# A second product scheme for w_down's other columns, in part of the rows, and plain steps into its banks

## The chip, the cores and the metric

The kernel runs on one core of a Trainium2 chip. The metric is the device time in microseconds; the kernel before takes 2009.6 us (median of 3 runs, 2009.06 to 2009.94). The engines are TensorE (PE: matmuls, PEld: its weight loads), VectorE (DVE), ScalarE (ACT), GpSimd (POOL) and SyncE (SP, which here only issues DMAs). Matmul sums land in PSUM banks of 128 x 512 fp32 values, from where DVE or ACT read them; the operands lie in SBUF.

## The reference

A two-layer bidirectional encoder over 256 tokens of width 2048, in fp32. Each layer has an attention part with three kinds of heads, and then the MLP, where this change is:

```
h = rmsnorm(x, norm_mlp[l])
u = relu(h @ w_up[l])          # 256 x 8192
x = x + (u * u) @ w_down[l]    # 8192 x 2048
```

## The kernel before

**Precision.** Each fp32 operand of a matmul is split into a high and a low part of the faster type fp32r. A product a·b is taken as three: high·high, low·high and high·low. For weights the split is made on the chip, step by step: ACT casts the tile to `whi` (L992), DVE subtracts to get `wlo` (L993).

**Steps.** Nearly all weight work is a list `steps`, one weight tile of 512 KB each, walked in order by the loop at the end of `tile_trunk`. At step i the loop issues the loads up to step i + 6 (`LOOK_LOAD`), the splits up to step i + 2 (in the MLP), the preparations `prep` up to step i + 4 (`LOOK_PREP`), and then the step's matmuls. `whi` and `wlo` have three buffers, the loaded tiles `wraw` five, `side` four, and `spare0` and `spare1` one each. The framework turns this into instructions for each engine, adds the waits, and may place an instruction that is ready ahead of one that isn't; so the order on an engine need not be the written one.

**The MLP in groups.** The 8192 inner columns are worked in eight groups g of 1024. `up_steps(g)` makes 16 steps that give the squared activations `uT[q]`, four tiles q per group with the high and the low part of 256 inner columns for all 256 tokens; an evaluation chain of ACT and DVE instructions follows every fourth step, and `sums_of` forms from the same values four sums of quarters, `sT[q]`, for the scheme below.

**Down in two ways.** The 2048 output columns fall into four blocks j of 512. For j = 2 and 3 `down_steps` is plain: per step 12 matmuls (two token halves t, two row blocks, three parts; `mode_b`, L465), into one bank per token half; after the group's last step DVE adds both banks to x (L720). For j = 0 and 1 `strassen_steps` uses seven products in place of eight (Winograd's form): the 2 x 2 block matrix has the two token halves as rows of the left side, two sets of inner rows between, and the columns j = 0 and j = 1 on the right. Each product P1 to P7 has two steps, for the two halves h of the group's rows, with 6 matmuls each (L787). The left operands are parts of `uT` (A11, A12, A22) or of `sT` (S1 to S4). The right operands come from the four weight blocks B11, B12, B21, B22:

- P1 loads B11 into a `spare` tile. As soon as it is split, an accumulating DMA issued from POOL adds B12 to it (`on_top`, in P2's `prep`).
- P2 takes B21 as it is.
- P7 loads B12 and B22 into `side` tiles; DVE adds them (L808).
- P6 takes B22 plus the spare tile, a DVE add (L814) into a `big` tile; when it is split, another accumulating DMA adds B21 (P5's `prep`). P4 takes that sum.
- P5 takes the spare tile, P3 takes B22.

The products share three banks. `a` and `d` are the halves of the one PSUM tile `S` that `score_banks()` gives (a new one is asked for at P1), `b` is an ordinary bank. P1, P6, P5 and P3 accumulate on in `a`, P7 and P4 in `d`, P2 is alone in `b`. Between the products DVE adds the state of the bank to, or subtracts it from, a quarter of x (`evac`, L763): once per product, at its second half.

**The order.** `order` merges the lists: 1 takes the next product step, 0 the next other step. In groups 0 to 5 the others are first 8 plain down steps (4 for j = 2, 4 for j = 3), then the 16 up steps of group g + 1. Each product stands as `1 0 1`, with two or three zeros up to the next product; two zeros come first. Groups 6 and 7 are ordered apart, and the last two groups' plain columns are done in group 7. A group of 0 to 5 has 38 steps.

Of the kernel before, what the change touches and what calls it, by code (L numbers as in the profile page):

```python
# [17 lines left out]
F32 = mybir.dt.float32  # L18
# [5 lines left out]
P = 128  # L24
# [19 lines left out]
def tile_trunk(ctx: ExitStack, tc: tile.TileContext, x_in, xt_in, w_in, w_o, w_up, w_down,  # L44
               gains, rowp, t5, rpb, gfin, cst, onehot, out):
    nc = tc.nc
    LOOK_LOAD, LOOK_SPLIT, LOOK_PREP, BUDGET = 7, 2, 5, 2.2
# [26 lines left out]
    def spare(dt, h):  # L74

        return wp.tile([P, 2, 512], dt, tag=f"spare{h}", bufs=1, name=nm("spare"))
# [4 lines left out]
    def mm_bank():  # L81
        return pp.tile([P, 512], F32, tag="bank", bufs=6, name=nm("mm"))
# [4 lines left out]
    def score_banks():  # L87
        return pp.tile([P, 4, 256], F32, tag="S", bufs=1, name=nm("S"))
# [5 lines left out]
    x = cp.tile([P, NT, D], F32, name="x")  # L94
# [356 lines left out]
    steps = []  # L451

    class Step:


        def __init__(self, src, kk, n, pre, mm, fourth=True, loads=None, prep=None, raw=None, post=None):
            self.src, self.kk, self.n, self.pre, self.mm, self.fourth = src, kk, n, pre, mm, fourth
            self.loads, self.prep, self.raw, self.post = loads or [], prep, raw, post

    def mode_b(banks, h_tile, wh, wl, sub, first, last, n=512, blocks=(0, 1), lo_last=False):  # L460

        def one(t, i, part):
            kk = sub[i]
            a = h_tile[i][:, int(part == "lh"), kk, t * P:(t + 1) * P]
            nc.tensor.matmul(banks[t][:, 0:n], a, (wl if part == "hl" else wh)[:, i, :],  # L465
                             start=first and i == 0 and part == "hh",
                             stop=last and i == len(sub) - 1 and part == stop)
        if lo_last:
            stop = "hl"
            for part in ("hh", "lh", "hl"):  # L470
                for t in blocks:
                    for i in range(len(sub)):
                        one(t, i, part)
            return
        stop = "lh"
        for t in blocks:
            for i in range(len(sub)):
                for part in ("hh", "hl", "lh"):
                    one(t, i, part)
# [3 lines left out]
    def layer_steps(l):  # L483
# [97 lines left out]
        ti = 0  # L581
# [114 lines left out]
            nc.vector.tensor_sub(t[:, 1], sm, f(t[:, 0]))  # L696
            sT[q] = t

        def down_steps(gs, j):

            out_, box = [], {}
            tiles = [(g, k) for g in gs for k in range(4)]
            final = l == L - 1 and gs == (7,)
            for n, (g, k) in enumerate(tiles):
                def mm(wh, wl, g=g, k=k, n=n):
                    last = n == len(tiles) - 1
                    if n == 0:
                        box["b"] = [mm_bank(), mm_bank()]
                        box["w"] = []
                    hts = [uT[4 * g + k]] * 2  # L710
                    mode_b(box["b"], hts, wh, wl, [0, 1], n == 0, last, blocks=(0,) if final else (0, 1),
                           lo_last=gs != (7,))
                    if final:
                        box["w"].append((hts, wh, wl))
                    if not last:
                        return

                    def evac(t):
                        xs = x[:, t, j * 512:(j + 1) * 512]
                        nc.vector.tensor_add(xs, xs, box["b"][t])  # L720
                    if final:
                        evac(0)
                        final_block(0)
                        tail = [mm_bank(), mm_bank()]
                        for c in range(2):
                            cols = slice(c * 256, c * 256 + 256)
                            for i, (hts, vh, vl) in enumerate(box["w"]):
                                mode_b([None, tail[c]], hts, vh[:, :, cols], vl[:, :, cols], [0, 1],
                                       i == 0, i == 3, n=256, blocks=(1,))
                            xs = x[:, 1, 1536 + c * 256:1792 + c * 256]  # L730
                            nc.vector.tensor_add(xs, xs, tail[c][:, 0:256])
                            square_cols(1, 1536 + c * 256, 256, fin["ss"][:, 7 + c:8 + c])
                        final_block(1)
                        return
                    evac(0)
                    evac(1)
                    if gs[-1] == 7:
                        layer_end(l, j)
                out_.append(Step(w_down[l, (g * 4 + j) * 4 + k], 2, 512, None, mm, fourth=gs == (7,)))
            return out_  # L740

        def strassen_steps(g):

# [2 lines left out]
            raw, t2, box, done = {}, {}, {}, set()  # L748

            def src(par, j, h):  # L750
                return w_down[l, g * 16 + (par * 2 + j) * 2 + h]

            def left(name, q):

# [3 lines left out]
                return [sT[q][:, i, "3124".index(name[1]), :] for i in range(2)]  # L758

            def evac(bank, t, j, sign):  # L760
                xs = x[:, t, j * 512:(j + 1) * 512]
                op = nc.vector.tensor_add if sign > 0 else nc.vector.tensor_sub
                op(xs, xs, bank)  # L763

# [8 lines left out]
                nc.gpsimd.dma_start(tile, src(par, j, h).rearrange("p (k n) -> p k n", k=2), accum_op=ALU.add)  # L773
            out_ = []
            for name, lf, bk, fresh, dst in plan:
                for h in range(2):
                    def mm(wh, wl, name=name, lf=lf, bk=bk, fresh=fresh, dst=dst, h=h):
                        if (name, h) == ("P1", 0):
                            pair = score_banks().rearrange("p (b i) n -> p b (i n)", i=2)
                            box["a"], box["d"] = pair[:, 0], pair[:, 1]  # L780
                        if (name, h) == ("P2", 0):
                            box["b"] = mm_bank()
                        o = box[bk]
                        ops = [left(lf, 2 * h + i + 4 * g) for i in range(2)]
                        for a, w in ((0, wh), (1, wh), (0, wl)):
                            for i in range(2):
                                nc.tensor.matmul(o, ops[i][a], w[:, i, :], skip_group_check=True,  # L787
                                                 start=fresh and h == 0 and i == 0 and a == 0 and w is wh,
                                                 stop=h == 1 and i == 1 and w is wl)
                        if h == 1:  # L790
                            evac(o, *dst)

                            if g == 7 and name in ("P3", "P4"):
                                layer_end(l, dst[1])
                    loads, prep, get = [], None, None
                    if name == "P1":
                        loads = [(("B11", h), src(0, 0, h), lambda h=h: spare(F32, h))]
                        get = lambda h=h: raw["B11", h]
                    elif name == "P2":
                        def prep(h=h):  # L800
# [25 lines left out]
                    def operand(get=get, key=(name, h)):  # L826
                        done.add(key)
                        return get()
                    stp = Step(src(1, 0, h) if name == "P2" else None, 2, 512, None, mm, fourth=False, prep=prep,
                               raw=operand if get else None,  # L830
                               loads=[(raw, k, v, w) for k, v, w in loads])
                    out_.append(stp)
            return out_

        steps.extend(up_steps(0))
        for g in range(8):

            if g < 6:
                ss = down_steps((g,), 2) + down_steps((g,), 3) + up_steps(g + 1)
            elif g == 6:  # L840
                ss = up_steps(7)
            else:
                ss = down_steps((6, 7), 2) + down_steps((6,), 3) + down_steps((7,), 3)
            hs = strassen_steps(g)

            order = [0, 0]
            for p_ in range(7):
                order += [1, 0, 1]
                if p_ < 6:
                    order += [0] * (2 if g < 6 else g == 6) + [0] * (g != 6 and p_ in (1, 3, 5))  # L850
            order += [0] * (len(ss) - order.count(0))
            assert order.count(0) == len(ss) and order.count(1) == len(hs), (order.count(0), order.count(1))
            steps.extend(hs.pop(0) if o else ss.pop(0) for o in order)

# [174 lines left out]
    for i, s in enumerate(steps):  # L1029
# [17 lines left out]
        while ns < min(len(steps), i + LOOK_SPLIT + (not s.fourth)):  # L1047
            split(ns)
            ns += 1
        while npr < min(len(steps), i + LOOK_PREP):  # L1050
            if steps[npr].prep:
                steps[npr].prep()
            npr += 1
# [67 lines left out]
def _pack_down(w, g):  # L1121

    plain = [_pack(w[:, j * 512:(j + 1) * 512], 2) for j in range(4)]
    b = w.reshape(8, P, D)
    plain[0:2] = [np.stack([b[[4 * h + par, 4 * h + par + 2], :, j * 512:(j + 1) * 512].transpose(1, 0, 2).reshape(P, 1024)
                            for j in range(2) for h in range(2)]) for par in range(2)]
    return np.concatenate(plain)


# [58 lines left out]
```

## Time and profile before

| | us |
|---|---|
| median of 3 runs | 2009.6 |
| the profiled execution | 2009.43 |
| its span, first to last instruction | 2007.7 |
| PE busy in the span | 1992.7 |
| DVE busy | 1599.0 |
| ACT busy | 1217.3 |

The page's chain of work that ended last covers only the final 34 us, from 1974.02 on. For the rest, windows and timelines of single groups are read. A window's row gives its limits and length, then for PE, PEld, DVE, ACT and POOL the busy time and the number of instructions, then the granted clock, the share of the DMA engines and GB/s. A timeline's row gives start, length, engine, line, operation, out<-in, form and how many were merged; in brackets the idle time ahead of it and what ended it. A record's length can reach past the start of the next one on the same engine, so paces are taken from starts.

### The profile page before, as it was taken

The page shows a single profiled execution, that of the slowest core. Times are in us where ns is not written, and L with a number is a line of the kernel's source. Part 1 is how long each engine was busy: PE and PEld are TensorE (multiplying, and loading weights), DVE is VectorE, ACT ScalarE, POOL GpSimd, SP SyncE. Part 2 cuts the span into 40 slices and gives each one's busy share as a digit, 9 for nine tenths or more (in the row PEclk, how much of TensorE's full clock was granted, in tenths as well). Part 3 has the DMA queues.
Part 4 walks back from the last instruction along what each step waited for, and adds up shares of the span by engine and source line. Part 5 has one row for each costly group of instructions (what it writes and reads, how often), then busy time and mean ns, then how long its engine had stood idle before and what let it go on. Part 6 is the DMA issues. An engine that isn't in the chain of part 4 may idle for free. (4 is left out here: it accounts for less than half of the span.)

```text
span 2007.7 us, 28054 instructions
## 1 busy us (share of the span) xinstructions
PE 1992.7 (99%) x10206; PEld 1698.4 (85%) x10206; DVE 1599.0 (80%) x2110; ACT 1217.3 (61%) x1745; POOL 348.2 (17%) x400
## 2 busy tenths in 40 slices
PE   9999999999999999999999999999999999999998
PEld 7888888888888888888888888888888888888886
DVE  7777877888888788888857688778888888888986
ACT  7667756565655656566657677565655556565664
POOL 0674620000000000000008655100000000000002
PEclk9999999999999999999999999999999999999999
DMA  9745655768776786768666465567687776877773
GB/s 345 212 158 159 213 166 189 216 208 242 211 233 214 213 233 208 239 209 237 204 186 195 147 191 187 175 193 218 207 248 212 232 209 206 246 213 234 205 237 129
DMA packets 118838, 420.62 MB, mean 210 GB/s; under 512 B 13571, under 2 KB 15875, under 8 KB 118700
## 3 DMA queue, kind: packets, MB, share of 16 engines
q1 hardware_dynamic: 109052, 384.18, 58.5%
q0 software_dynamic: 9216, 33.56, 10.1%
q8 instruction: 80, 1.31, 0.3%
q10 hardware_dynamic: 432, 1.10, 0.1%
q14 instruction: 58, 0.48, 0.1%
HBM read 412.99 MB, written 2.11 MB: 207 GB/s over the span
## 5 line engine op out<-in xcount | busy, mean ns | idle before, releaser
L993 DVE TENSOR_TENSOR wlo<-wraw,whi 128x1024 fp32r<-128x1024 f32 (+1 forms) x553 | 683.1, 1237 | 240.9 <-ACT whi L992 238.1
L992 ACT CAST whi<-wraw 128x1024 fp32r<-128x1024 f32 (+1 forms) x553 | 579.8, 1050 | 454.7 <-PE mm L465 170.8
L465 PE MATMUL mm<-whi,big 128*128 128x512 f32 (+1 forms) x2172 | 613.1, 385 | 0.2 <-ACT whi L992 0.2
L670 PE MATMUL mm<-big,whi 128*128 128x512 f32 x2048 | 509.6, 391 | 0.0
L465 PEld LDWEIGHTS mm<-whi,big 128*128 128x128 f32 x2172 | 404.2, 188 | 79.8 <-ACT whi L992 1.3
L670 PEld LDWEIGHTS mm<-big,whi 128*128 128x128 f32 x2048 | 377.6, 188 | 74.5
L465 PE MATMUL mm<-wlo,big 128*128 128x512 f32 (+1 forms) x1086 | 355.4, 384 | 1.3 <-DVE wlo L993 1.3
L675 PEld LDWEIGHTS mm<-big,wlo 128*128 128x128 f32 x2048 | 279.4, 190 | 20.0
L675 PE MATMUL mm<-big,wlo 128*128 128x256 f32 x2048 | 285.5, 282 | 0.0
L465 PEld LDWEIGHTS mm<-wlo,big 128*128 128x128 f32 x1086 | 204.2, 188 | 39.6 <-DVE wlo L993 1.6
L787 PE MATMUL S<-whi,big 128*128 128x512 f32 x768 | 209.1, 394 | 0.8 <-DVE x L763 0.8
L773 POOL DMA_DIRECT2D spare<-in_w_down_dram x32 | 28.0, 876 | 745.8 <-DVE wlo L993 671.2
L787 PEld LDWEIGHTS S<-whi,big 128*128 128x128 f32 x768 | 134.9, 189 | 22.2 <-DVE x L763 2.0
L465 PE MATMUL mm<-spare,big 128*128 128x512 f32 (+1 forms) x606 | 140.2, 380 | 0.0
L465 PEld LDWEIGHTS mm<-spare,big 128*128 128x128 f32 x606 | 108.9, 188 | 20.5
L787 PE MATMUL S<-wlo,big 128*128 128x512 f32 x384 | 118.8, 391 | 0.0
L773 POOL DMA_DIRECT2D big<-in_w_down_dram x32 | 27.7, 866 | 492.3 <-DVE wlo L993 485.5
L992 ACT CAST whi<-big 128x1024 fp32r<-128x1024 f32 x64 | 67.2, 1050 | 70.6 <-PE mm L670 50.4
L992 ACT CAST whi<-side 128x1024 fp32r<-128x1024 f32 x64 | 67.2, 1051 | 65.4 <-PE mm L670 41.2
L993 DVE TENSOR_TENSOR wlo<-big,whi 128x1024 fp32r<-128x1024 f32 x64 | 79.3, 1239 | 33.4 <-ACT whi L992 33.3
L992 ACT CAST whi<-spare 128x1024 fp32r<-128x1024 f32 x64 | 67.4, 1053 | 52.1 <-PE mm L670 40.7
L993 DVE TENSOR_TENSOR wlo<-side,whi 128x1024 fp32r<-128x1024 f32 x64 | 78.5, 1227 | 23.7 <-ACT whi L992 23.3
(154 smaller groups left out, 2108.4 us busy)
## 6 DMA issues: line engine op xcount, KB each, us to landing
wraw<-in_w_up_dram SPq DMA_DIRECT2D x256, 512.0 KB, 4.4
wraw<-in_w_down_dram SPq DMA_DIRECT2D x160, 512.0 KB, 4.1
wraw<-in_w_in_dram SPq DMA_DIRECT2D x119, 512.0 KB, 3.7
wraw<-in_w_o_dram SPq DMA_DIRECT2D x64, 512.0 KB, 3.7
side<-in_w_down_dram SPq DMA_DIRECT2D x64, 512.0 KB, 4.4
spare<-in_w_down_dram SPq DMA_DIRECT2D x32, 512.0 KB, 4.4
spare<-in_w_down_dram POOLq DMA_DIRECT2D x32, 512.0 KB, 5.8
big<-in_w_down_dram POOLq DMA_DIRECT2D x32, 512.0 KB, 6.7
```

The costliest lines, as they stand in the source:

```text
L465: nc.tensor.matmul(banks[t][:, 0:n], a, (wl if part == "hl" else wh)[:, i, :], start=first and i == 0 and part == "hh", stop=last and i == ...
L670: nc.tensor.matmul(box["b"][fs], wh[:, kk, fs * P:(fs + 1) * P], ht, start=s == 0 and kk == 0, stop=False, skip_group_check=True)
L675: nc.tensor.matmul(box["b"][fs][:, 0:256], wl[:, kk, fs * P:(fs + 1) * P], ht[:, 0:256], start=False, stop=s == 3 and kk == 3, skip_group_ ...
L773: nc.gpsimd.dma_start(tile, src(par, j, h).rearrange("p (k n) -> p k n", k=2), accum_op=ALU.add)
L787: nc.tensor.matmul(o, ops[i][a], w[:, i, :], skip_group_check=True, start=fresh and h == 0 and i == 0 and a == 0 and w is wh, stop=h == 1 ...
L992: last_act[0] = nc.scalar.copy(h[:, part], w[:, part]).ins
L993: last_lo[0] = nc.vector.tensor_sub(lo[:, part], w[:, part], f(h[:, part])).ins
```

## The change

In groups 0 to 5 the columns j = 2 and 3 get products too, but only for the group's first 512 inner rows (`uT` q = 0 and 1): `strassen_steps(g, 1, (0,), ...)` makes seven steps, one for each product. The other 512 rows (k = 2 and 3) stay plain: `down_steps((g,), 3, (2, 3))` with banks of its own, and `down_steps((g,), 2, (2, 3), shared)`, whose two steps add on to the open banks `b` (P2) and `d` (P7 and P4) of the new products and finish them with two adds. So P2 and P4 of the new set have no evac of their own.

The order of a group is new, 41 steps in all. Written out by position, P for a product step of the first set, P' of the second:

- 0 to 24: P1 and P2 as `P up P up`; P7 as `P j3 P j3` (the two plain steps for j = 3); P6 as `P up P`; P5 as `P up P up`; P3 as `P up P`; P4 as `P up P`, with one up step between P5 and P3 and none between P6 and P5 or P3 and P4 (positions 14, 15 and 21, 22);
- 25 to 38: seven times `up P'`;
- 39 and 40: the two plain steps for j = 2.

P6 of the new set is prepared one step later than others (`look` 4). P1 of the new set loads into `spare1`. The weights are packed anew on the host so that each step still finds its tile in one piece. `skip_group_check` is a flag for the build only.

```diff
-        def down_steps(gs, j):
+        def down_steps(gs, j, ks=range(4), shared=None):
...
-            tiles = [(g, k) for g in gs for k in range(4)]
+            tiles = [(g, k) for g in gs for k in ks]
...
-                        box["b"] = [mm_bank(), mm_bank()]
+                        box["b"] = [shared["b"], shared["d"]] if shared else [mm_bank(), mm_bank()]
...
-                    mode_b(box["b"], hts, wh, wl, [0, 1], n == 0, last, blocks=(0,) if final else (0, 1),
+                    mode_b(box["b"], hts, wh, wl, [0, 1], n == 0 and not shared, last, blocks=(0,) if final else (0, 1),
...
-        def strassen_steps(g):
+        def strassen_steps(g, pair=0, tiles=(0, 1), look=(LOOK_PREP, LOOK_PREP)):
...
-                for h in range(2):
+                for h in tiles:
...
-                        if h == 1:
+                        if h == tiles[-1] and not (pair and name in ("P2", "P4")):
                             evac(o, *dst)
...
             if g < 6:
-                ss = down_steps((g,), 2) + down_steps((g,), 3) + up_steps(g + 1)
+                up = up_steps(g + 1)
+                ss = up[0:4] + down_steps((g,), 3, (2, 3)) + up[4:]
...
-            hs = strassen_steps(g)
...
-            order = [0, 0]
-            for p_ in range(7):
-                order += [1, 0, 1]
-                if p_ < 6:
-                    order += [0] * (2 if g < 6 else g == 6) + [0] * (g != 6 and p_ in (1, 3, 5))
-            order += [0] * (len(ss) - order.count(0))
+            hs, _ = strassen_steps(g)
+            if g < 6:
+                more, shared = strassen_steps(g, 1, (0,), (LOOK_PREP, 4))
+                hs += more
+
+            if g < 6:
+                order = []
+                for p_ in range(7):
+                    order += [1, 0, 1] + [0] * (p_ in (0, 1, 2, 4))
+                order += [0, 1] * 7 + [0, 0]
+                ss += down_steps((g,), 2, (2, 3), shared)
...
-        while npr < min(len(steps), i + LOOK_PREP):
+        while npr < len(steps) and npr < i + steps[npr].look:
```

More of the change, by code (lines that the diff above doesn't have):

```diff
@@ L453, in tile_trunk, with __init__ @@
     class Step:
-        def __init__(self, src, kk, n, pre, mm, fourth=True, loads=None, prep=None, raw=None, post=None):
+        def __init__(self, src, kk, n, pre, mm, fourth=True, loads=None, prep=None, raw=None, post=None,
+                     look=LOOK_PREP):
+            self.look = look
             self.src, self.kk, self.n, self.pre, self.mm, self.fourth = src, kk, n, pre, mm, fourth
@@ L466, in one @@
                              start=first and i == 0 and part == "hh",
-                             stop=last and i == len(sub) - 1 and part == stop)
+                             stop=last and i == len(sub) - 1 and part == stop, skip_group_check=True)
         if lo_last:
@@ L738, in mm @@
                         layer_end(l, j)
-                out_.append(Step(w_down[l, (g * 4 + j) * 4 + k], 2, 512, None, mm, fourth=gs == (7,)))
+                ti = (g * 4 + j) * 4 + k if g >= 6 else g * 16 + 12 + (j - 2) * 2 + k - 2
+                out_.append(Step(w_down[l, ti], 2, 512, None, mm, fourth=gs == (7,)))
             return out_
-        def strassen_steps(g):
+        def strassen_steps(g, pair=0, tiles=(0, 1), look=(LOOK_PREP, LOOK_PREP)):
             raw, t2, box, done = {}, {}, {}, set()
             def src(par, j, h):
-                return w_down[l, g * 16 + (par * 2 + j) * 2 + h]
+                return w_down[l, g * 16 + ((par * 2 + j) * 2 + h if pair == 0 else 8 + par * 2 + j)]
             def left(name, q):
@@ L760, in evac @@
             def evac(bank, t, j, sign):
-                xs = x[:, t, j * 512:(j + 1) * 512]
+                xs = x[:, t, 1024 * pair + j * 512:1024 * pair + (j + 1) * 512]
                 op = nc.vector.tensor_add if sign > 0 else nc.vector.tensor_sub
@@ L775, in strassen_steps @@
             for name, lf, bk, fresh, dst in plan:
-                for h in range(2):
+                for h in tiles:
                     def mm(wh, wl, name=name, lf=lf, bk=bk, fresh=fresh, dst=dst, h=h):
                         if (name, h) == ("P1", 0):
-                            pair = score_banks().rearrange("p (b i) n -> p b (i n)", i=2)
-                            box["a"], box["d"] = pair[:, 0], pair[:, 1]
+                            two = score_banks().rearrange("p (b i) n -> p b (i n)", i=2)
+                            box["a"], box["d"] = two[:, 0], two[:, 1]
                         if (name, h) == ("P2", 0):
@@ L788, in mm @@
                                                  start=fresh and h == 0 and i == 0 and a == 0 and w is wh,
-                                                 stop=h == 1 and i == 1 and w is wl)
-                        if h == 1:
+                                                 stop=h == tiles[-1] and i == 1 and w is wl)
+                        if h == tiles[-1] and not (pair and name in ("P2", "P4")):
                             evac(o, *dst)
@@ L796, in strassen_steps @@
                     if name == "P1":
-                        loads = [(("B11", h), src(0, 0, h), lambda h=h: spare(F32, h))]
+                        loads = [(("B11", h), src(0, 0, h), lambda h=h + pair: spare(F32, h))]
                         get = lambda h=h: raw["B11", h]
@@ L829, in strassen_steps @@
                     stp = Step(src(1, 0, h) if name == "P2" else None, 2, 512, None, mm, fourth=False, prep=prep,
+                               look=look[name == "P6"],
                                raw=operand if get else None,
@@ L832, in strassen_steps @@
                     out_.append(stp)
-            return out_
+            return out_, box
         steps.extend(up_steps(0))
@@ L843, in layer_steps @@
                 ss = down_steps((6, 7), 2) + down_steps((6,), 3) + down_steps((7,), 3)
-            hs = strassen_steps(g)
-            order = [0, 0]
-            for p_ in range(7):
-                order += [1, 0, 1]
-                if p_ < 6:
-                    order += [0] * (2 if g < 6 else g == 6) + [0] * (g != 6 and p_ in (1, 3, 5))
-            order += [0] * (len(ss) - order.count(0))
+            hs, _ = strassen_steps(g)
[8 more added lines that the diff above has]
+                ss += down_steps((g,), 2, (2, 3), shared)
+            else:
+                order = [0, 0]
+                for p_ in range(7):
+                    order += [1, 0, 1]
+                    if p_ < 6:
+                        order += [0] * (g == 6) + [0] * (g == 7 and p_ in (1, 3, 5))
+                order += [0] * (len(ss) - order.count(0))
             assert order.count(0) == len(ss) and order.count(1) == len(hs), (order.count(0), order.count(1))
@@ L1126, in _pack_down @@
                             for j in range(2) for h in range(2)]) for par in range(2)]
+    if g < 6:
+        plain[2:4] = [np.stack([b[[par, par + 2], :, j * 512:(j + 1) * 512].transpose(1, 0, 2).reshape(P, 1024)
+                                for par in range(2) for j in (2, 3)]), plain[2][2:4], plain[3][2:4]]
     return np.concatenate(plain)
```

## The prediction

> **What bounds the kernel now.** I read the page's busy shares first, then the waits, then windows over single groups of the MLP, then the timeline of TensorE (PE) and VectorE (DVE) inside them.
>
> ```profile
> span 2007.7 us, 28054 instructions
> PE 1992.7 (99%) x10206; PEld 1698.4 (85%) x10206; DVE 1599.0 (80%) x2110; ACT 1217.3 (61%) x1745; POOL 348.2 (17%) x400
> PEclk9999999999999999999999999999999999999999
> PEld S L787 <- DVE x L763: 2.0, 3, 1.2
> ```
>
> PE is busy 99% of the span at full granted clock, so time goes only if PE gets fewer matmuls or starts to wait. The last row is from the waits: weight loads of product matmuls (L787) waited three times, 2.0 us in all, for a VectorE instruction that adds a finished bank into x (L763, an "evac" below). That wait matters later.
>
> ```profile
> 617.88:703.38 85.50, 85.50 (x438) 73.11 (x436) 69.82 (x86) 49.14 (x59) 3.49 (x4) 1.00 0.74 222
> 874.41:938.07 63.66, 63.66 (x341) 55.05 (x340) 57.90 (x75) 40.47 (x49) 3.49 (x4) 1.00 0.78 233
> ...
> 562.36 1.09 PE L787 MATMUL S<-whi,big 128*128 128x512 f32 x4
> 563.75 1.98 PE L670 MATMUL mm<-big,whi 128*128 128x512 f32 x8
> 566.51 1.09 PE L787 MATMUL S<-whi,big 128*128 128x512 f32 x4
> ...
> 623.33 1.07 PE L787 MATMUL S<-whi,big 128*128 128x512 f32 x4
> 624.68 1.98 PE L465 MATMUL mm<-whi,big 128*128 128x512 f32 x8
> 627.40 1.07 PE L787 MATMUL S<-whi,big 128*128 128x512 f32 x4
> ```
>
> The first two rows are windows (length, then busy time of PE, weight loads, DVE, ACT, POOL; clock; DMA share; GB/s): one group of 0 to 5, and group 6. PE has no gap in either. The rows below are starts of steps: product step plus up step 4.15 us, a down step 627.40 - 624.68 = 2.72 us, thus 2.72 / 12 = 0.2267 us for a 512-column matmul, and 1.36 us for a product step of six. (The records' 0.39 us overlap; only distances between starts count.)
>
> **What PE saves.** Per group, 8 down steps of 12 matmuls (96) become 7 product steps of 6 (42) and 4 down steps of 12 (48): 90. Six matmuls of 0.2267 us are 1.36 us; 12 groups (0 to 5, two layers) give **-16.3 us**. 85.50 becomes 84.1 us a group.
>
> The Trainium skill, page "TensorE: Matmul & The Clock Gate", section "Back-to-back issue gap", gives about 131 ns for each 512-column matmul in a stream of loads and matmuls; by it the saving would be only 72 x 0.131 = 9.4 us, an estimate. The rows above show 227 ns with the loads in between, so I do not use it.
>
> **What DVE gains in work.** A split (L993) per step: 38 become 41. Adds that form a second operand (L808, L814): 4 become 6. Evacs: 7 + 4 become 7 + 5 + 2 + 2 = 16, since two products of the new set are left in banks that the last down steps finish. The chains after the up steps stay.
>
> ```profile
> 643.93 1.22 DVE L808 TENSOR_TENSOR side<-side,side 128x1024 f32<-128x1024 f32 x1
> 645.07 1.28 DVE L720 TENSOR_TENSOR x<-x,mm 128x512 f32<-128x512 f32 x2
> ...
> 664.58 0.42 DVE L691 TENSOR_TENSOR mid<-mid 128x256 f32<-128x256 f32 x1
> 664.91 0.69 DVE L656 TENSOR_TENSOR big<-mid,big 128x512 fp32r<-128x512 f32 x1
> 665.51 0.29 DVE L692 SCALAR_TENSOR_TENSOR mid<-mid,mid 128x128 f32<-128x128 f32 x1
> 665.72 0.68 DVE L763 TENSOR_TENSOR x<-x,S 128x512 f32<-128x512 f32 x1
> ...
> 689.57 0.74 DVE L649 TENSOR_TENSOR mid<-mid,mm 128x256 f32<-128x256 f32 x2
> 690.23 0.68 DVE L763 TENSOR_TENSOR x<-x,S 128x512 f32<-128x512 f32 x1
> 690.83 0.68 DVE L650 SCALAR_TENSOR_TENSOR mid<-mid,rrow 128x512 f32<-128x512 f32 x1
> 691.43 1.22 DVE L993 TENSOR_TENSOR wlo<-wraw,whi 128x1024 fp32r<-128x1024 f32 x1
> 692.58 1.23 DVE L993 TENSOR_TENSOR wlo<-big,whi 128x1024 fp32r<-128x1024 f32 x1
> 693.86 0.69 DVE L656 TENSOR_TENSOR big<-mid,big 128x512 fp32r<-128x512 f32 x1
> ...
> 900.31 1.23 DVE L814 TENSOR_TENSOR big<-side,spare 128x1024 f32<-128x1024 f32 x1
> 917.67 1.23 DVE L993 TENSOR_TENSOR wlo<-side,whi 128x1024 fp32r<-128x1024 f32 x1 [0.20 <-ACT whi L992]
> ```
>
> Start to start, with the next one waiting: add 1.14 us, split about 1.14, evac 0.60, L649 pair 0.66, L650 0.60, L691 0.33, L656 0.60, L692 0.21; L693 is taken like L692 and L696 like L656. A chain is 0.66 + 0.60 + 0.33 + 0.60 + 0.21 + 0.21 + 0.60 = 3.2 us, four per group. Before: 38 x 1.14 + 4 x 1.14 + 11 x 0.60 + 12.8 = 67.3 of 85.5 us (79%). After: 41 x 1.14 + 6 x 1.14 + 16 x 0.60 + 12.8 = 75.9 of 84.1 us (**90%**). By stretch, from the new order of the 41 steps:
> - steps 0 to 24 (14 products, 9 up, 2 down): PE 9 x 4.15 + 2 x 4.07 + 3 x 1.36 = 49.6; DVE 25 x 1.14 + 4.6 + 9 x 0.60 + 2 x 3.2 = 44.9 (91%);
> - steps 25 to 38 (7 up, 7 products): PE 29.1; DVE 14 x 1.14 + 2.3 + 5 x 0.60 + 6.4 = 27.6 (95%);
> - steps 39 and 40: PE 5.4; DVE 2.3 + 1.2 = 3.5.
>
> None passes PE. Is 90% sustainable? Group 6 by the same sum: 30 x 1.14 + 4.6 + 7 x 0.60 + 12.8 = 55.8 of 63.66 us, 88%, with no PE gap, and from 900.31 to 917.47 DVE ran 17 us without a gap, PE still full. Added step by step (a step's DVE work less its PE time, never below zero), DVE's queue in the new order is longest in two places: 0.9 us after step 12, then 1.14 + 3.2 - 2.79 for step 13 with a chain and 1.14 + 0.60 - 1.36 for step 14 make 2.8 us; and from zero after step 28, 2 x 1.14 + 3.2 - 2.79 for step 29 and 0.4 for step 30 make 3.1 us. Splits run two steps ahead of their use, some 4.15 us, so both queues fit. So I cost the DVE work at nothing; it costs 12 us for each us per group that it falls short. ACT gains 3 casts of 1.05 us on 49.14 us a group: hidden likewise.
>
> The Trainium skill, page "VectorE: DVE Perf Modes", section "The DRAIN you can't avoid", says that the next VectorE instruction doesn't start before the pipe has emptied. The whole record would then be the cost: 41 x 1.23 + 6 x 1.22 + 16 x 0.68 + 4 x 3.8 = 83.8 of 84.1 us, an estimate, and the DVE rival below would be the likeliest case. The rows (records 1.22 us, starts 1.14 apart) speak against it.
>
> **Waits that the new order adds.** (a) P6's last step (14) now stands right ahead of P5's first (15), both in bank a: P5 waits for P6's evac. (b) P3's last (21) ahead of P4's first (22): other halves of the tile S. (c) At the end of a group the last down step (40) leaves an open bank of S, and the next group's P1 needs a new S: it waits for two evacs; ten such borders (group 6 begins with up steps). (d) At group 0, P1's second half needs the last up evac, only 4.15 us behind. On PE, everything is queued behind such a matmul. Before has such neighbours in group 7:
>
> ```profile
> 962.58 1.52 PE L465 MATMUL mm<-whi,big 128*128 128x512 f32 x6
> 963.32 0.68 DVE L763 TENSOR_TENSOR x<-x,S 128x512 f32<-128x512 f32 x1
> 964.06 1.21 PE L787 MATMUL S<-whi,big 128*128 128x512 f32 x4
> ...
> 977.36 1.98 PE L465 MATMUL mm<-whi,big 128*128 128x512 f32 x8
> 979.18 1.09 PE L787 MATMUL S<-whi,big 128*128 128x512 f32 x4
> ...
> 1968.14 4.19 POOL L874 TENSOR_TENSOR x<-x,big 128x512 f32<-128x512 f32 x2 [6.06 <-ACT mid L881]
> 1971.27 2.14 DVE L993 TENSOR_TENSOR wlo<-wraw,whi 128x1024 fp32r<-128x1024 f32 x1
> 1974.06 1.20 PE L787 MATMUL S<-whi,big 128*128 128x512 f32 x4 [0.78 <-DVE x L763]
> ```
>
> At 962.58 P7's last step has ended and P6's first is due; it waits for P7's evac although that reads the other bank, which is why I count (b). But the framework moved six matmuls of the next down step in front: 962.58 + 6 x 0.2267 = 963.94, the product starts at 964.06, **0.12 us lost**. At 977.36 (P5, then P3, the same bank) eight were moved and nothing is lost. At 1974.06, 0.78 us is lost, but there a split took 2.14 us beside POOL's work on x, which groups 0 to 5 don't have (POOL has 4 entries of 0.87 us in the window of the group, all DMA issues). For (a) to (d) the steps that can be moved in front are up steps of 2.76 us, and the DVE queue is at most 2.8 us. Bounds: 0 and 0.78 us each (28 us in all); I take 0.12, the nearest row, for 12 + 12 + 10 + 2 = 36 places: **+4.3 us**. For (d) without cover: the chain took from 688.10 (the step's end) to 693.86 + 0.69, 6.4 us, so 2.3 us twice.
>
> **DMA.** Two more accumulating transfers from POOL and 1 MB more a group, 20 of about 85 us, on a share of 0.74; group 6 ran at 0.78.
>
> ```profile
> DMA to landing us min/median/max: 5.3/6.6/9.1
> 621.35 0.87 POOL L773 DMA_DIRECT2D spare<-in_w_down_dram  x1 [45.12 <-DVE wlo L993]
> ```
>
> The issue at 621.35 came 2.0 us ahead of its P1 step (623.33). In the new set the sum P6 needs it must start at latest 9.8 us behind P1's start (three pairs of 4.15 us and 0.9 us of matmuls, less 3.5 us for add, cast and split): 11.8 us for a landing of at most 9.1. SP's loads wait for the splits that free their buffers (spare1 by P5's second half, nine steps ahead of its use). Cost nothing; without the 2.7 us of cover, 12 us for each us.
>
> **The sum.** The profiled execution took 2009.43 us: 2009.43 - 16.3 + 4.3 = 1997.4; it lies 0.2 us under the median of 2009.6, so I forecast **1997.6 us**.
>
> **Rivals.**
> - *Bank waits stay open.* If the order on PE stays as written, (a) and (b) cost 964.06 - 962.58 = 1.48 us each, (c) 1.28 us (the two evacs at 645.07), (d) 2.3: 24 x 1.48 + 10 x 1.28 + 2 x 2.3 = 53 us, 2046 us, slower. It turns from a mean wait of 16.3 / 36 = 0.45 us on. For: the order is made anew at build time. Against: all three undisturbed neighbours were filled. Partly filled (0.3 us each): 2004.
> - *DVE becomes the bound.* If its gaps can't shrink under group 6's share (12%), a group takes 75.9 / 0.88 = 86.3 us, +2.2 x 12: 2024 us; it turns from a share of 75.9 / 85.5 = 89% on. For: DVE waits for ACT's casts in nearly every step. Against: 17 us without a gap. In part (0.5 us a group): 2003.6.
> - *Late sums.* An accumulating DMA 1 us later than its cover: +12, 2009.6 us. Against: 2.7 us of cover.
> - *The matmuls saved are worth less*, as by the issue-gap rule: 2009.6 - 9.4 + 4.3 = 2004.5. Against: 227 ns in every step.
>
> **How the numbers follow.** Forecast (1993.3 without any wait, to 2001) 0.70; bank waits 0.12, half of it partly filled; DVE 0.10, a third of it in part; late DMA 0.05; smaller saving 0.03. Range **1993 to 2005**: it leaves out the open bank waits, the full DVE bound and the late DMA, some 0.17. A measurement can tell 0.2% (4 us) from no change: faster (under 2005.6) 0.82, same 0.09, slower 0.09.
>
> **What would show it.** Window of a group 84.1 to 84.6 us, with 432 matmuls in place of 438 in the same count; some 10 more DVE records and its wait for ACT's casts about halved; PE gaps only ahead of L787 matmuls released by an evac, 0.1 us each, with up matmuls (L670) split around P5, P4 and P1. Wrong if PE waits on splits (L993) inside steps 25 to 38, if those gaps reach 0.45 us, or if POOL's sums release a cast.

## The result and the profile after

The changed kernel takes **2015.82 us** (median of 7 runs, 2014.64 to 2016.86), the kernel before, run beside it, 2009.6 us (7 runs, 2009.06 to 2010.33). The ratio is 1.0028, with a 95% interval of 1.0019 to 1.0038: slower by about 6 us, where 12 us less had been forecast. The profiled execution took 2014.88 us, its span is 2013.0 us.

Two rows of the page of the changed kernel first, then two windows of it (length; busy time and instructions of PE, PEld, DVE, ACT, POOL; clock; DMA share; GB/s). The first window is one whole group, the second is positions 26 to 38 of that group.

```profile
span 2013.0 us, 28191 instructions
...
PE 1986.2 (99%) x10134; PEld 1680.8 (83%) x10134; DVE 1692.9 (84%) x2230; ACT 1250.3 (62%) x1781; POOL 369.0 (18%) x424
```

```profile
446.79:532.76 85.97, 84.95 (x432) 71.68 (x430) 77.71 (x97) 51.92 (x62) 5.24 (x6) 1.00 0.76 232
500.90:527.32 26.42, 26.42 (x141) 22.74 (x139) 24.63 (x29) 15.86 (x21) 0.88 (x1) 1.00 0.79 246
```

The page alone would mislead: PE has 72 matmuls fewer (10134 against 10206) and is busy 6.5 us less, and its share is 99% as before. The group's window says where to look. A group has its 432 matmuls, 6 fewer, as planned, and lasts 85.97 us: longer than the 85.50 of before, and 1.9 us longer than the 84.1 that 6 matmuls fewer should give. PE is idle for 1.02 us of it, and none of this lies in the second window: the fullest stretch (DVE 24.63 of 26.42 us, 93%) has no gap. Positions 39 and 40 have none either (PE 5.44 of 5.44 us). So the loss is ahead of position 26. The waits of the changed kernel name it (engine and line that waited, for what; us in total, times, longest):

```profile
PE S L793 <- ACT whi L1010: 11.1, 12, 1.0
...
PEld S L793 <- ACT whi L1010: 21.7, 24, 1.4
...
ACT whi L1010 <- DVE big L820: 39.8, 29, 2.4
```

Twelve waits, one for each group of 0 to 5 in two layers, 1.0 us at most and 11.1 in all: a product's matmul waits for ACT's cast of its weights, and ACT's casts wait for a VectorE add, L820 (L814 in the kernel before). That add makes the right operand of P6. The timeline of the changed kernel around the place, VectorE, ACT and PE (rows between are left out):

```profile
463.39 1.09 PE L793 MATMUL S<-whi,big 128*128 128x512 f32 x4
...
464.91 0.74 DVE L651 TENSOR_TENSOR mid<-mid,mm 128x256 f32<-128x256 f32 x2
...
465.64 1.23 DVE L1011 TENSOR_TENSOR wlo<-wraw,whi 128x1024 fp32r<-128x1024 f32 x1
...
466.79 0.68 DVE L652 SCALAR_TENSOR_TENSOR mid<-mid,rrow 128x512 f32<-128x512 f32 x1
...
468.26 0.43 DVE L693 TENSOR_TENSOR mid<-mid 128x256 f32<-128x256 f32 x1 [0.79 <-ACT mid L655]
...
468.93 0.68 DVE L658 TENSOR_TENSOR big<-mid,big 128x512 fp32r<-128x512 f32 x1
...
469.74 0.68 DVE L769 TENSOR_TENSOR x<-x,S 128x512 f32<-128x512 f32 x1
...
470.33 1.22 DVE L820 TENSOR_TENSOR big<-side,spare 128x1024 f32<-128x1024 f32 x1
...
470.67 1.07 PE L467 MATMUL mm<-wlo,big 128*128 128x512 f32 x4
...
471.64 1.04 ACT L1010 CAST whi<-big 128x1024 fp32r<-128x1024 f32 x1 [1.17 <-DVE big L820]
...
472.74 1.19 PE L793 MATMUL S<-whi,big 128*128 128x512 f32 x4 [1.00 <-ACT whi L1010]
...
473.77 0.66 PE L672 MATMUL mm<-big,whi 128*128 128x512 f32 x2
...
474.27 0.62 PE L793 MATMUL S<-wlo,big 128*128 128x512 f32 x2
...
474.73 1.53 PE L672 MATMUL mm<-big,whi 128*128 128x512 f32 x6
...
476.27 0.50 PE L793 MATMUL S<-whi,big 128*128 128x512 f32 x1
```

From the bottom up: the last matmuls of the step before end at 470.67 + 4 x 0.2267 = 471.58, P6 starts at 472.74: **1.16 us lost**. Behind it the parts of P6 and of the next up step come piecewise, with another 0.1 to 0.2 us lost at several starts (474.73 + 6 x 0.2267 = 476.09, the next start is 476.27). P6 waited for the cast at 471.64, the cast for the add at 470.33. From the start of the add to the product are 2.41 us, so the add should have started by 469.17. What stood ahead of it on VectorE from 464.91 on is an up chain, L651, L652, L693 to L695 and L658, with a stop of 0.79 us in it for ACT. Two instructions that are written behind the add stand ahead of it as well: the split of position 11 (465.64) and P7's evac of position 10 (469.74). In the kernel before, the same add and the same chain stand the other way round, as three rows of its timeline show:

```profile
651.25 1.22 DVE L814 TENSOR_TENSOR big<-side,spare 128x1024 f32<-128x1024 f32 x1
...
655.40 1.22 DVE L814 TENSOR_TENSOR big<-side,spare 128x1024 f32<-128x1024 f32 x1
...
660.46 0.75 DVE L649 TENSOR_TENSOR mid<-mid,mm 128x256 f32<-128x256 f32 x2
```

Both adds of P6 are over almost 4 us before the group's first chain (L649 there, L651 after) begins. The new order has the fourth up step at position 7 and P6 at 12 and 14, with the adds issued four positions ahead, at positions 8 and 10: behind the chain.

### The profile page after: what moved, and what is told of

Its sections match the earlier page's. It is cut to its first block, busy times and chain, and to the rows that moved or that the text cites. A ratio compares the mean times of both kernels' runs of the same rounds, so it can differ in the third digit from the quotient of the medians.

```text
span 2013.0 us, 28191 instructions
## 1 busy us (share of the span) xinstructions
PE 1986.2 (99%) x10134; PEld 1680.8 (83%) x10134; DVE 1692.9 (84%) x2230; ACT 1250.3 (62%) x1781; POOL 369.0 (18%) x424
## 5 line engine op out<-in xcount | busy, mean ns | idle before, releaser
L1011 DVE TENSOR_TENSOR wlo<-wraw,whi 128x1024 fp32r<-128x1024 f32 (+1 forms) x517 | 636.1, 1236 | 189.9 <-ACT whi L1010 177.2
L1010 ACT CAST whi<-wraw 128x1024 fp32r<-128x1024 f32 (+1 forms) x517 | 540.9, 1050 | 354.5 <-PE mm L672 100.1
L467 PE MATMUL mm<-whi,big 128*128 128x512 f32 (+1 forms) x1692 | 500.4, 385 | 0.7 <-ACT whi L1010 0.7
L467 PEld LDWEIGHTS mm<-whi,big 128*128 128x128 f32 x1692 | 314.1, 188 | 62.2 <-ACT whi L1010 2.3
L793 PE MATMUL S<-whi,big 128*128 128x512 f32 x1056 | 294.0, 397 | 12.5 <-ACT whi L1010 11.1
L467 PE MATMUL mm<-wlo,big 128*128 128x512 f32 (+1 forms) x846 | 293.2, 382 | 1.3 <-DVE wlo L1011 1.3
L793 PEld LDWEIGHTS S<-whi,big 128*128 128x128 f32 x1056 | 183.7, 189 | 54.9 <-ACT whi L1010 21.7
L467 PEld LDWEIGHTS mm<-wlo,big 128*128 128x128 f32 x846 | 159.2, 188 | 30.3 <-DVE wlo L1011 1.6
L793 PE MATMUL S<-wlo,big 128*128 128x512 f32 x528 | 163.5, 391 | 0.0
L793 PEld LDWEIGHTS S<-wlo,big 128*128 128x128 f32 x528 | 99.2, 188 | 22.2
```

The lines of the kernel that those rows point to most:

```text
L1010: last_act[0] = nc.scalar.copy(h[:, part], w[:, part]).ins
L1011: last_lo[0] = nc.vector.tensor_sub(lo[:, part], w[:, part], f(h[:, part])).ins
```

## The experiments

Two theories after that reading. **Q**: it is the order of VectorE's queue; P6's adds and casts stand behind the chain, and the rest of the change is worth what was forecast. **T**: VectorE is simply too full with the second set of products; the wait at P6 is where that shows.

**The chain later.** The changed kernel, but the first chain of each group goes behind the fifth up step, position 13, by the means that the kernel already has for each layer's first tile:

```diff
-                        if s == 3 and q > 0:
+                        if s == 3 and q % 4:
...
-                                     post=evacs[0] if (q, s) == (1, 0) else None))
+                                     post=evacs[0] if (q % 4, s) == (1, 0) else None))
```

> In the changed kernel, the evaluation chain of the first up tile of each group 0 to 6 is put behind the fifth up step (position 13) instead of behind the fourth (position 7); nothing is left out. Theory Q (a local queue: this chain stands ahead of P6's adds on VectorE): the wait of 1.0 us ahead of P6's first product goes in all 12 groups and with it the restarts around it, a group falls from 85.95 to about 84.3 us, time 1996 to 2000 us. Rival T (VectorE is too full all over the group, the wait only shows where): the wait comes back at P5, P3 or in the second set, time 2011 to 2016 us.

Measured: **1996.84 us** (4 runs, 1996.28 to 1996.91), ratio to the kernel before 0.9933 (0.9918 to 0.9948). A window of one group and the timeline around P6 in this run:

```profile
446.91:531.20 84.29, 84.29 (x431) 71.90 (x430) 77.52 (x97) 51.94 (x62) 5.24 (x6) 1.00 0.79 237
```

```profile
465.04 1.22 DVE L820 TENSOR_TENSOR big<-side,spare 128x1024 f32<-128x1024 f32 x1
...
467.31 0.74 DVE L651 TENSOR_TENSOR mid<-mid,mm 128x256 f32<-128x256 f32 x2
...
469.20 1.22 DVE L820 TENSOR_TENSOR big<-side,spare 128x1024 f32<-128x1024 f32 x1
...
477.23 1.52 PE L672 MATMUL mm<-big,whi 128*128 128x512 f32 x6
...
478.59 1.08 PE L793 MATMUL S<-whi,big 128*128 128x512 f32 x4
```

The first add now stands ahead of the chain, the second behind only the chain's first pair of instructions (L651); PE is busy for the whole of the group's 84.29 us, and VectorE does the same work as in the changed kernel (97 instructions, 77.5 us) in a shorter group. The last two rows are a bank neighbour, P6's second half and P5: six up matmuls were put between, 477.23 + 6 x 0.2267 = 478.59, and nothing is lost. Theory Q holds, T doesn't.

**The adds earlier.** The changed kernel with its chain in place, but with the look of the first set's P6 raised from 5 to 7. The loop prepares the steps in their order, and the step in front of each P6 step keeps its 5, so the adds are issued one position earlier, at 7 and 9 in place of 8 and 10 (two steps were expected). Position 7 still puts the first add ahead of the chain, which follows that position's matmuls:

```diff
-            hs, _ = strassen_steps(g)
+            hs, _ = strassen_steps(g, look=(LOOK_PREP, 7 if g < 6 else LOOK_PREP))
```

> In the changed kernel, P6's adds of the first set are issued two steps earlier (look 7 in place of 5), so the first add stands ahead of the chain and the second still behind it. Theory Q: the wait ahead of P6's first half goes, a smaller one (under 1 us) appears at its second half: 2001 to 2009 us. Rival T: no change, 2013 to 2017 us.

Measured: 2002.46 us (2002.16 to 2003.55), ratio 0.9963 (0.9948 to 0.9978). Most of the loss is gone, but not all. The timeline of this run around both adds and at P6's second half, then the window of a group:

```profile
463.46 1.22 DVE L820 TENSOR_TENSOR big<-side,spare 128x1024 f32<-128x1024 f32 x1
...
464.59 0.74 DVE L651 TENSOR_TENSOR mid<-mid,mm 128x256 f32<-128x256 f32 x2
...
472.94 1.22 DVE L820 TENSOR_TENSOR big<-side,spare 128x1024 f32<-128x1024 f32 x1
...
474.24 1.05 ACT L1010 CAST whi<-big 128x1024 fp32r<-128x1024 f32 x1 [1.17 <-DVE big L820]
...
475.32 1.22 DVE L1011 TENSOR_TENSOR wlo<-big,whi 128x1024 fp32r<-128x1024 f32 x1
...
475.54 1.09 PE L793 MATMUL S<-whi,big 128*128 128x512 f32 x4
...
476.60 0.73 PE L793 MATMUL S<-wlo,big 128*128 128x512 f32 x2
```

```profile
446.39:531.37 84.98, 84.98 (x432) 71.72 (x430) 77.59 (x98) 51.69 (x62) 5.24 (x6) 1.00 0.79 235
```

The first half's add got ahead of the chain, the second half's did not. Its split starts at 475.32, and the product's low part, due at 475.54 + 4 x 0.2267 = 476.45, waits till 476.60; more is lost after it. A group of this run takes 84.98 us from border to border, and the window shows PE busy for all of it: the records reach over short waits, so a full PE row alone doesn't prove that nothing is lost. The distances between starts and the length of the group decide.

**Fewer evacs.** The changed kernel without the five adds into x that follow products of the new set (its output lacks what they add; the two adds behind the last plain steps stay), which takes five VectorE instructions of 0.60 us out of each group and leaves the order:

```diff
-                        if h == tiles[-1] and not (pair and name in ("P2", "P4")):
+                        if h == tiles[-1] and not pair:
```

> The changed kernel without the five adds into x of the second set's products (their part of x is left out): VectorE has 3 us less work a group, all of it behind P6 of the first set. Theory Q: the wait at P6 stays at 1 us, time 2012 to 2016 us. Rival T: the load falls from 90 to 87% and the time by at least half of what was lost, under 2006 us.

Measured: 2015.47 us (2015.15 to 2016.36), ratio 1.0028 (1.0017 to 1.0038): the time of the changed kernel, with the wait of L793 for the cast as it was, twelve times, 11.1 us. Three us less work for VectorE in a group bought nothing. The five adds all stand behind P6, at positions 26 to 36, so the run speaks against a VectorE that is too full over the whole group; it doesn't change what stands right ahead of P6. The next run does more against T.

**The order alone.** The kernel before, all plain steps kept, with only the new order of the first 25 positions; the plain steps that are left come at the group's end (block 3 is summed in two pieces, which makes two more adds into x a group):

```diff
-                ss = down_steps((g,), 2) + down_steps((g,), 3) + up_steps(g + 1)
+                up = up_steps(g + 1)
+                ss = (up[0:4] + down_steps((g,), 3, (2, 3)) + up[4:]
+                      + down_steps((g,), 3, (0, 1)) + down_steps((g,), 2))
...
+                if g < 6:
+                    order += [1, 0, 1] + [0] * (p_ in (0, 1, 2, 4))
+                    continue
```

> The kernel before with the changed kernel's order of the first 25 steps of a group, without the second set of products: columns 2 and 3 stay plain (two steps of block 3 in the same places, the other six behind the up steps). VectorE's work per group is that of before and two more adds into x (about 80% of the time). Theory Q, which blames the order at P6 and not the load: the wait at P6 is there too, 12 x 1.6 us, time 2024 to 2030 us. Rival T: no wait, 2009 to 2012 us.

Measured: **2029.62 us** (2028.3 to 2029.78), ratio 1.0095 (1.0078 to 1.0112). Its waits and its timeline at P6:

```profile
PE S L787 <- ACT whi L997: 11.1, 12, 1.0
```

```profile
472.42 1.22 DVE L814 TENSOR_TENSOR big<-side,spare 128x1024 f32<-128x1024 f32 x1
...
473.72 1.04 ACT L997 CAST whi<-big 128x1024 fp32r<-128x1024 f32 x1 [1.17 <-DVE big L814]
...
474.82 1.20 PE L787 MATMUL S<-whi,big 128*128 128x512 f32 x4 [1.00 <-ACT whi L997]
```

The same wait, 11.1 us in twelve places, without one product of the new set, and with VectorE busy for 1611.0 us, 79% of the span, where the kernel before has 1599.0 us and 80%. This speaks most plainly against T. The order alone costs 2029.62 - 2009.82 (the kernel before, beside it) = 19.8 us, more than the saved matmuls are worth.

**The order alone, with the chain later.** The same kernel with the two edited lines of the first experiment:

> The kernel before with the new order of the first 25 steps (as in the run of the order alone), and the chain of the group's first up tile moved from position 7 to position 13. Theory Q (order of VectorE's queue: the chain stands ahead of the adds that form P6's operand): the order alone cost 19.8 us over the kernel before, 1.65 us for each of 12 groups; with the chain behind the adds the wait ahead of P6's first product is gone and what stays are the bank neighbours, 0 to 0.3 us a group: 2009.6 to 2013 us, and no wait of L787 for ACT's cast above 0.5 us inside groups. Rival B (the loss of the order alone comes from its bank neighbours P6/P5 and P3/P4, or from the two plain steps between the products): stays at 2025 to 2030 us.

Measured: 2010.55 us (11 runs, 2010.23 to 2011.41), ratio 1.0004 (0.9995 to 1.0012). Of the 19.8 us, 0.9 us are left, and L787 is no longer among the matmuls that wait for ACT's cast. So neither the bank neighbours nor the plain steps between the products were the price: it was the chain ahead of the adds.

**Two placings of the free steps.** Two runs put the free steps between P7, P6, P5, P3 and P4, where two products share a bank or a tile, and let P1, P2 and P7 stand close; one with the chain later, one with the chain left where the changed kernel has it:

```diff
-                    order += [1, 0, 1] + [0] * (p_ in (0, 1, 2, 4))
+                    order += [1, 0, 1] + [0] * (p_ in (2, 3, 4, 5))
```

> The changed kernel with the first chain moved behind the fifth up step, and with the free steps placed between P7 and P6, P6 and P5, P5 and P3, P3 and P4 in place of P1 and P2, P2 and P7, P7 and P6, P5 and P3. The two neighbours on one bank or tile (P6/P5, P3/P4) are gone. The step-wise queue of VectorE stays at or under 2.1 us. If the bank neighbours still cost 0.12 us each in the run with the later chain (1996.84 us), 24 of them give -2.9 us: 1993 to 1995 us. If they cost nothing: 1996 to 1998 us. Against it, the first three products stand close together, and if the sum that P6 needs from the accumulating DMA or P7's adds come late there, it is slower than 1999 us, with PE waiting ahead of P7 or P6.

> The same placing of the free steps, but the first chain left where the changed kernel has it (behind the fourth up step, now position 9 in place of 7). P6's adds are now issued at positions 6 and 8, ahead of that chain, and the step-wise queue still reaches 3.5 us after position 9. Theory Q (what counts is that the adds and casts for P6 stand behind the chain, not the length of the queue by itself): the wait ahead of P6 is gone or under 0.3 us, 1993 to 1999 us. If a queue of 3.5 us costs by itself: PE waits for splits at positions 10 to 13, 0.4 to 1 us a group, 2000 to 2007 us. If the chain isn't the cause at all: 2013 to 2017 us as the changed kernel.

Measured: 1995.43 us with the chain later (5 runs, 1993.8 to 1995.78; ratio 0.9927, 0.9914 to 0.9941), and **1994.82 us** with this one line alone (5 runs, 1994.06 to 1995.32; ratio 0.9925, 0.9913 to 0.9937). These two are not told apart. A window of a group and the timeline of the latter:

```profile
446.49:530.70 84.21, 84.21 (x431) 71.90 (x430) 77.33 (x97) 51.80 (x62) 5.24 (x6) 1.00 0.80 237
```

```profile
446.49 1.75 PE L672 MATMUL mm<-big,whi 128*128 128x512 f32 x7
...
448.08 1.09 PE L793 MATMUL S<-whi,big 128*128 128x512 f32 x4
...
460.58 1.21 DVE L820 TENSOR_TENSOR big<-side,spare 128x1024 f32<-128x1024 f32 x1
...
464.13 1.22 DVE L820 TENSOR_TENSOR big<-side,spare 128x1024 f32<-128x1024 f32 x1
...
466.05 1.15 PE L793 MATMUL S<-whi,big 128*128 128x512 f32 x4
...
467.00 0.74 DVE L651 TENSOR_TENSOR mid<-mid,mm 128x256 f32<-128x256 f32 x2
```

Here the fourth up step is at position 9 and P6 at 10 and 12, so the adds are issued at positions 6 and 8. They lie at 460.58 and 464.13, the chain starts at 467.00: the order of the kernel before is back, without moving a chain. The step-wise queue still reaches 3.5 us after position 9, and PE shows no wait of a product for a cast. What counts is which instruction stands behind it. This run beats both kernels, by 14.9 us against the one before.

## Why the prediction was wrong, point by point

- **The saving on PE was right.** 1.36 us a group was forecast; in the last run a group takes 84.21 us against 85.50, with PE full in both: 1.29 us, or 0.215 us for each of the six matmuls. By the Trainium skill's rule ("TensorE: Matmul & The Clock Gate", "Back-to-back issue gap") of about 131 ns each it would be 0.79 us, an estimate. That run has more than that, and its whole gain, 2009.68 - 1994.82 = 14.9 us, is far above the 9.4 us that the rule gave. The row decided. The same section of the Trainium skill gives about 216 ns as the spacing of a single, isolated matmul. That lies near the runs (0.2267 us from start to start).
- **The failed step is the step-wise queue of VectorE**, at "0.9 us after step 12, then 1.14 + 3.2 - 2.79 for step 13 with a chain". That chain is at position 7. I had read the line that takes the chain of a tile to the next tile's first step (`post`, where (q, s) is (1, 0)) as holding for each group's first tile. It holds for each layer's first tile only; for all others the chain comes right behind the fourth up step. With the chain in its place the same sum gives 1.5 us after position 6, then 1.5 + 1.14 + 3.2 - 2.79 = 3.1 after 7, 4.0 after 8, 3.9 after 10, and still 3.3 at P6 itself.
- **A second omission goes with it.** I held every queue against "splits run two steps ahead of their use, some 4.15 us" and counted L820 as work of 1.14 us like any other. But P6's operand goes from add to cast before it can be used: in the trace 2.41 us from the add's start to the product. A queue of 3.5 us ahead of plain splits cost no such wait in the last run. The redone sum names the place, but even it doesn't give the wait: position 8 starts at 463.39, and 3.1 us of queue and a split of 1.14 put the add at 467.6, ahead of the 469.17 by which it was due. It started at 470.33, because the stop of 0.79 us for ACT and the two instructions written behind it, a split and an evac, came first as well (467.6 + 0.79 + 1.14 + 0.60 = 470.1). The price is clear: the changed kernel differs from the last run by 2015.82 - 1994.82 = 21.0 us over 12 groups, 1.75 us each; the windows say 85.97 - 84.21 = 1.76 us, of which the first wait is 1.16.
- **"I cost the DVE work at nothing" was right in amount**, though not in order. A DVE share of 90% was worked out; the windows have 77.71 / 85.97 (90%) in the changed kernel and 77.33 / 84.21 (92%) in the last run, the latter without a PE gap. The rival by which VectorE becomes the bound (2024 us, "in part" 2003.6) would have come nearer to the time, but its mechanism isn't what happened: the order alone lost 19.8 us with the load of before, and 3 us less of evacs changed nothing. The Trainium skill's page "VectorE: DVE Perf Modes" ("The DRAIN you can't avoid") would have filled a group with 83.8 us of VectorE work, an estimate from whole records. The windows, with VectorE busy for 77 to 78 us of a group, don't bear that out. That page of the Trainium skill limits the rule, in "Two Vector instructions with no wait between them", to instructions that are held. The rows agree with that: starts 1.14 us apart beside records of 1.22.
- **The bank waits (+4.3 us) were over-counted.** At the shown places the neighbours and borders were filled without any gap: 477.23 to 478.59 in the run with the later chain, and at the border in the last run 446.49 + 7 x 0.2267 = 448.08. Taking the neighbours P6/P5 and P3/P4 away moved 1996.84 to 1995.43 us, at most 0.06 us for each of 24 places where I took 0.12. All that the new order costs by itself, once the chain is out of the way, is 0.9 us (2010.55 against 2009.68).
- **DMA cost nothing, as forecast.** The sums of P6 were issued at 443.69 and 449.64, and no accumulating transfer of this run took more than 9.2 us to land, so they were there by 458.8; the first add started at 470.33. ACT's casts waited for L820, and for no transfer of `w_down` or `w_up` (the only transfers that they waited for, 2.7 us in all, bring `w_in` tiles).
- **What the prediction named as its own disproof:** PE waits for splits inside positions 25 to 38 did not come, nor gaps of 0.45 us released by an evac in groups 0 to 5 (the one of 0.78 us, at 1978.80, is in group 7, as in the kernel before), nor POOL's sums as a releaser. VectorE's wait for ACT's casts fell from 318.4 to 215.9 us, by a third where about half had been named. The wait that came, on ACT's cast of an operand that VectorE forms first, was not on that list, and among the rivals there was none with a late operand other than the accumulating DMA's.

What stays open: the last run is still some 1.5 us above 2009.6 - 16.3 = 1993.3 us; no single place was found for that. Nor does a run show why the framework put the split of position 11 and P7's evac ahead of the add in the changed kernel; in every run that brought the first add ahead of the chain, the wait of 1.0 us ahead of P6 was gone.

## What to carry to other kernels

An operand that passes through two engines before its matmul has its own due time: hold the queue ahead of *its first instruction* against that, not the average lead of the others. Before a share of busy time is read as safe or as full, list, for the new order, what is issued right ahead of each such instruction, and read the conditions in the code that decide at which step a long chain is issued. Then check the list against the order that the build made, which need not be the written one. A queue can be moved by placing other work: one list of four indices was worth 21 us here, more than three times what the change had lost.

## What the runs showed that I had not expected

- VectorE at 92% of a group (77.33 of 84.21 us) beside a PE without a gap, and at 93% in positions 26 to 38 of the changed kernel. Taking 3 us of VectorE work out of a group that waits moved the time by 2015.82 - 2015.47 = 0.35 us, within the runs' spread.
- A wait of 1.0 us on PE cost 1.76 us in its group. The wait itself was 1.16 us by the starts, and the rest went in small restarts behind it, where product and up matmuls were fed in pieces of 1, 2, 3 and 6.
